# Sparse-attention layer of a two-layer streaming encoder: when index queries take up 1/rms, where values are projected, and which engine scales late softmaxes

## The chip, the cores and the metric

The kernel runs on one core of a Trainium2 chip. Its time is device microseconds of one execution, measured over several executions. A profile records one execution, and every row of a view comes from that one.

The engines have names of their own in the views: PE is TensorE (matmuls), PEld its weight loads, DVE is VectorE, ACT is ScalarE, POOL is GpSimd, SP is SyncE, which issues most transfers here. A q behind a name is the engine's queue of DMA issues.

## The reference, cut to what matters

One inference step over 512 prompt frames and 64 sample frames goes through two layers: a pooling mixer with an MLP, then sparse attention with an MLP. The change lies in the attention. Each query ranks the keys with a small indexer (8 heads of 64), keeps the best 256 at most, and attends to these with 16 heads in 4 groups.

```python
p = rmsnorm(x, g) @ w_in            # q 1024, k 256, v 256, qi 512, ki 64, wi 8
q, k, qi, ki = rope(q), rope(k), rope(qi), rope(ki)
wi = p[..., -8:] * 8 ** -0.5
logits = einsum('bthd,bsd->bths', qi, ki) * 64 ** -0.5
score = einsum('bths,bth->bts', relu(logits), wi)
_, idx = top_k(where(adm, score, NEG), n_sel)
s = einsum('btgrd,btkgd->btgrk', qg, k[idx]) * 64 ** -0.5
p = softmax(where(valid, s, NEG))
o = einsum('btgrk,btkgd->btgrd', p, v[idx])
return o @ w_o
```

The projections are linear, so the factor 1/rms of each frame can be left out of x and multiplied in later. relu is also linear in a positive factor: relu(r * y) is r * relu(y).

## The kernel before, in words

Activations lie transposed, 128 features by 576 frames (512 prompt, then 64 sample). To keep precision every matmul operand is split in a high and a low part (`wh`/`wl` for weights, two halves of `xs` for activations), and each product is three matmuls. A matmul over 576 frames runs as two of 288. Weights come in blocks as `raw` tiles; the high part is a cast on ACT (L190), the low part a subtraction (L191) on DVE, or on POOL where `next_block(sub=pool)` or the kind of block says so. A scheduler places all instructions when the kernel is built: each engine gets one fixed order, and runs it in order, each instruction waiting for its inputs and buffers.

The attention layer is `attention` (L1099 on). In order of the code:

- Four blocks give the index queries (`pj` in PSUM). Blocks 0 and 1 are copied to SBUF by ACT (`copies`); statistics of the norm are started, and during the last block `spread()` (L1204) broadcasts 1/rms to `rb` and multiplies it into the rotation tables `cs` (POOL, L1211) and `sn` (DVE, L1212). `rope` (L1141) rotates a pair of blocks: four multiplies and two sums. `rope_qi(0, copies=...)` rotates the first four heads from the copies, `rope_qi(1, started=...)` the last four from PSUM (L1156). Each splits the result in two parts and sends it through DRAM to `qi` by SP (L1180 and L1185).
- Between the two stands the projection of index keys and weights (`pki`). `turnable` holds the weights times 1/rms (L1230); it is transposed by PE (L1247) to `wi`. The key gets the scaled tables.
- Then K and the four groups of q are projected and rotated, most of it on POOL (L1161 to L1170). Between their matmuls `pace()` lets in index scores from step `PACE_FROM` on (L1273, relu on ACT at L1274, weighted sum on DVE from L1277).
- `top_k` finds, for four blocks of queries of 192, 320, 448 and 576 keys, the mask: rounds of MAX8 (L1291) and MATCH_REPLACE8 (L1292), then a threshold (L1293) and two transfers that lay the mask out by 128 rows (L1295, L1296).
- Values are projected (L1527): five tiles `v` of 24 matmuls, each evicted by ACT with the factor `r` (L1530).
- `steps()` runs 40 units (query block i of 5, key group g of 4, pair of heads s of 2). i from 0 to 3 are prompt blocks of 128 queries with (i+1)*128 keys; i = 4 is the sample with 576 keys. `scores` of a unit runs three units (`AHEAD`) before its `transpose`. `softmax` is one DVE pass with the mask (L1311) and an exponential on ACT (L1312) that also sums the row. From i = 2 on `over` scales p by 1/sum: POOL raises the sum to -1 (L1318) and multiplies (L1320). For i below 2 the scaling comes after the values, on DVE. PE transposes p (L1367, L1372), ACT copies it to `pT`, and PE multiplies it with V (L1399, L1405).
- From unit 18 on, every other step runs one block of the output projection for the first 256 frames (`wa`, in `ahead_out`), with its lower splits on POOL.
- At the end POOL adds these to x, reloaded from DRAM (L1545), and the output projection of the other 320 frames (`wo`) follows.

Of the kernel before, what the change touches and what calls it, by code (L numbers as in the profile page):

```python
# [16 lines left out]
P = 128  # L17
D = 1024
KT = D // P
TP = 512  # L20
# [18 lines left out]
PACE_FROM = 12  # L39
# [18 lines left out]
def pool_dsa_kernel(ctx: ExitStack, tc: tile.TileContext, a, o):  # L58
# [1040 lines left out]
    def attention(parts):  # L1099
# [42 lines left out]
        def rope(fast, started=(), cast=act.copy, copies=()):  # L1142

            pts = list(started)
            while len(pts) < 2 and not copies:
                pt = psum("pj")
                project(pt, next_block(), xs, between)
                pts.append(bank_halves(pt))
            a2, b2 = (tmp("rp", "rp", 4) for _ in range(2))
            a1, b1 = copies or (tmp("rp", "rp", 4) for _ in range(2))  # L1150
            eng = dve if fast else pool
            if fast and not copies:
                pa, pb = pts
                for out, pt, by in ((a1, pa, cs), (a2, pa, sn), (b2, pb, sn), (b1, pb, cs)):
                    for t, half in pt:
                        dve.tensor_tensor(halves(out)[:, half], t, halves(by)[:, half], ALU.mult)  # L1156
            else:
                for out, pt in zip((a1, b1), pts):
                    for t, half in pt:
                        turned[:] = [act.copy(halves(out)[:, half], t).ins]  # L1160
                eng.tensor_tensor(a2, a1, sn, ALU.mult)  # L1161
                eng.tensor_tensor(a1, a1, cs, ALU.mult)
                eng.tensor_tensor(b2, b1, sn, ALU.mult)
                eng.tensor_tensor(b1, b1, cs, ALU.mult)
            eng.tensor_tensor(a1, a1, b2, ALU.subtract)
            eng.tensor_tensor(b1, b1, a2, ALU.add)
            st = [pair_slot("b", "st") for _ in range(2)]
            for j, t in enumerate((a1, b1)):
                cast(st[j][:, 0], t)
                low = pool.tensor_tensor(st[j][:, 1], t, f32(st[j][:, 0]), ALU.subtract)  # L1170
            turned.append(low.ins)
            return (a1, b1), st

        def rope_qi(g, **ready):

            _, st = rope(True, **ready)
# [20 lines left out]
        copies = []  # L1197
        for i in range(2):
            pt = psum("pj")
            project(pt, next_block(), xs)  # L1200
            copies.append(tmp("rp", "rp", 4))
            act.copy(halves(copies[i]), pt[:, :, :HT])
            if i == 0:
                norm.stats()  # L1204

        def spread():

            for k in range(KT):
                if k == SPREAD_AT:
# [5 lines left out]
        started = []  # L1215
        for i in range(2):
            pt = psum("pj")
            project(pt, next_block(), xs, spread() if i else iter(()))
            started.append(bank_halves(pt))
        r = norm.r  # L1220
        between = iter(())
        qi = const([P, NIDX, TP], "qi", F32R, phase["queries"])
        pool.memset(f32(qi[:, :, TP - P:TP - TS]), 0.0)
        rope_qi(0, copies=copies)
        pki = psum1("ki"), psum1("ki")
        project(pki, next_block(), xs)
        rope_qi(1, started=started)
        turnable = tmp("wi")
        for h, pk in enumerate(pki):
            dve.scalar_tensor_tensor(halves(turnable[0:32])[:, h], pk[64:96, :HT], NIDX ** -0.5, halves(norm.rb[0:32])[:, h], ALU.mult, ALU.mult)  # L1230
        t1, t2, ki = tmp("t1"), tmp("t2"), tmp("ki")
# [82 lines left out]
        def over(sums, *heads):  # L1314
# [3 lines left out]
            pool.tensor_tensor(rs, sums, inverse[:, :n], ALU.pow)  # L1318
            for h, p in enumerate(heads):
                pool.tensor_scalar(p, p, rs[:, h:h + 1], 1.0, ALU.mult, ALU.mult)  # L1320

        class Unit:
# [5 lines left out]
            def scores(self):  # L1328
# [6 lines left out]
                if i < 4:  # L1335
# [8 lines left out]
                    if i >= TURNED:  # L1344
                        over(self.group.sums[:, 2 * s:2 * s + 2], self.pr[:, 0], self.pr[:, 1])
                else:
# [6 lines left out]
                    over(self.group.sums[:, s:s + 1], self.pr)  # L1353
# [95 lines left out]
        def ahead_out():  # L1449

            for m in range(KT):
# [3 lines left out]
                with behind(turned):  # L1455
                    w = next_block(sub=pool)
# [11 lines left out]
        def steps():  # L1468
# [3 lines left out]
            for u in range(-AHEAD - 2, total + 2):  # L1472
# [5 lines left out]
                if 0 <= u + AHEAD < total:  # L1478
# [3 lines left out]
                    v.scores()  # L1482
                if 0 <= u - 1 < total:
# [5 lines left out]
                yield  # L1489

# [12 lines left out]
        act.activation(small(8, "e1", 1), wi[:, 1], AF.Exp)  # L1503
# [15 lines left out]
        wv = [next_block(), next_block()]  # L1519
        for i in range(5):  # L1520
            n = P if i < 4 else TS
            pt = psum1("v")
            for k in range(KT):
                wh, wl = wv[k // 4][k % 4 // 2]
                sl = slice((k % 2) * 256, (k % 2 + 1) * 256)
                for j, (part, wt) in enumerate(((0, wh), (1, wh), (0, wl))):
                    pe.matmul(pt[:n, :256], xs[k][:, part, i * P:i * P + n], wt[:, sl],  # L1527
                              start=(k == 0 and j == 0), stop=(k == KT - 1 and j == 2))
            vi = i if i < 4 else 8
            act.activation(V[:n, vi], pt[:n, :256], AF.Copy, scale=r[:n, i:i + 1])  # L1530
        nc.sync.dma_start(o["v_p"], V[:, 0:4])
        nc.sync.dma_start(o["v_s"], V[:TS, 8])
# [125 lines left out]
```

## Time and profile before

| | us |
|---|---|
| median of 3 runs (lowest, highest) | 1087.7 (1087.55, 1088.82) |
| the profiled execution's own time | 1087.32 |
| span of its profile | 1085.1 |
| PE busy in the span | 1053.3 (97%) |
| DVE busy | 893.0 (82%) |
| ACT busy | 631.3 (58%) |
| POOL busy | 258.2 (24%) |

The span leaves out 2.2 us that lie around it. The attention layer runs from about 409 to 696 us of the span, between the two MLPs. A busy time is the time in which an engine executed something; a wait shows in brackets behind the instruction that ended it, with what released it. PE's instructions are pipelined, so a busy PE may still run at a lower clock, and each window gives the clock that was granted.

### The profile page before, as it was taken

Reading aid. Unit: us, or ns where it says so; the run is one execution under the profiler, and the core shown is the slowest. Engines: PE = TensorE matmul, PEld = TensorE weight load, DVE = VectorE, ACT = ScalarE, POOL = GpSimd, SP = SyncE. Lnnn points to the kernel's source line nnn. Section 1 sums busy time; section 2 is a strip of 40 time slices with the busy share of each in tenths; the row PEclk is TensorE's granted clock in tenths of the full one; section 3 lists DMA queues with packets and bytes.
Section 4 is the critical chain, followed back from the end, with each engine's and each line's share of the span. In section 5 each row is a group of like instructions: output and inputs, shape, how many; then the busy total and the mean of one; then the engine's idle time right before and its main releaser. Section 6 shows DMA issues by size and latency. Waiting matters only on the chain.

```text
span 1085.1 us, 21735 instructions
## 1 busy us (share of the span) xinstructions
PE 1053.3 (97%) x7978; PEld 1028.0 (95%) x7978; DVE 893.0 (82%) x1822; ACT 631.3 (58%) x1262; POOL 258.2 (24%) x285
## 2 busy tenths in 40 slices
PE   8999999999999999989989999999999999999996
PEld 8999999999999999989988787999999999999995
DVE  7889889879979996859999433779989879978984
ACT  8556457447547764434378765646556547647741
POOL 3200111111111101576516784000111111111101
PEclk9999999999999999999989999999999999999999
DMA  8333666676676655675352443533666676576522
GB/s 250 91 103 89 170 166 151 175 167 164 147 184 165 158 169 173 183 194 162 104 172 79 141 138 109 159 98 90 161 164 163 160 174 168 146 182 162 127 60 88
DMA packets 98427, 160.17 MB, mean 148 GB/s; under 512 B 15777, under 2 KB 29584, under 8 KB 98320
## 3 DMA queue, kind: packets, MB, share of 16 engines
q1 hardware_dynamic: 71120, 112.30, 33.1%
q0 software_dynamic: 15840, 28.84, 16.8%
q10 hardware_dynamic: 11360, 17.63, 5.1%
q8 instruction: 63, 1.03, 0.4%
q14 instruction: 44, 0.36, 0.1%
HBM read 142.99 MB, written 12.72 MB: 143 GB/s over the span
## 4 chain that ended last, share of the span: by engine, by line
PE 85%; issue 4%; DVE 4%; POOL 2%; ACT 2%; DMA 2%; SPq 0%; DVEq 0%; ACTq 0%; POOLq 0%
PE b L522 32%; PE c L522 16%; PE up L320 9%; PE a L522 8%; PE pj L320 7%; PE wo L320 3%; PE wa L320 2%; PE pb L1066 1%; PE o L1399 1%; PE dn L320 1%; PE pt L1367 1%; PE ix L1269 1%; PE sc L1341 1%; PE ix L1273 1%; POOL p L1320 1%
## 5 line engine op out<-in xcount | busy, mean ns | idle before, releaser
L190 ACT CAST wh<-raw 128x512 fp32r<-128x512 f32 x316 | 194.6, 619 | 222.5 <-PE b L522 62.9
L191 DVE TENSOR_TENSOR wl<-raw,wh 128x512 fp32r<-128x512 f32 x284 | 199.1, 703 | 40.6 <-ACT wh L190 36.7
L522 PE MATMUL b<-u,wh 128*128 128x288 f32 x992 | 203.3, 296 | 2.3 <-ACT a L559 1.9
L522 PEld LDWEIGHTS b<-u,wh 128*128 128x128 f32 x992 | 159.6, 188 | 4.3 <-ACT a L559 3.1
L190 ACT CAST wh<-sum 128x512 fp32r<-128x512 f32 x165 | 102.3, 620 | 95.8 <-PE b L522 41.9
L522 PE MATMUL b<-u,wl 128*128 128x288 f32 x496 | 145.8, 295 | 0.4 <-DVE wl L191 0.4
L191 DVE TENSOR_TENSOR wl<-sum,wh 128x512 fp32r<-128x512 f32 x165 | 112.1, 685 | 22.4 <-ACT wh L190 20.8
L253 POOL DMA_DIRECT2D sum<-in_w_down x31 | 27.1, 893 | 331.0 <-DMA sum<-in_w_down 105.6
L522 PE MATMUL c<-u,wh 128*128 128x288 f32 x496 | 102.7, 296 | 0.0
L522 PEld LDWEIGHTS b<-u,wl 128*128 128x128 f32 x496 | 93.5, 189 | 0.6 <-DVE wl L191 0.6
L320 PE MATMUL up<-xs,wh 128*128 128x288 f32 x512 | 89.4, 296 | 0.2
L488 DVE TENSOR_TENSOR u<-v,u 128x576 fp32r<-128x576 f32 (+3 forms) x106 | 83.0, 785 | 2.1 <-ACT u L485 1.6
L522 PEld LDWEIGHTS c<-u,wh 128*128 128x128 f32 x496 | 79.7, 188 | 1.4 <-ACT wh L190 1.1
L522 PE MATMUL b<-xt,wh 128*128 128x288 f32 x384 | 77.7, 296 | 0.0
L522 PE MATMUL b<-xs,wh 128*128 128x288 f32 x384 | 77.2, 295 | 0.0
L485 ACT CAST u<-v 128x576 fp32r<-128x576 f32 (+3 forms) x106 | 73.7, 699 | 3.2 <-DVE v L509 2.2
L320 PEld LDWEIGHTS up<-xs,wh 128*128 128x128 f32 x512 | 74.7, 188 | 1.0 <-DVE v L474 0.6
L522 PE MATMUL c<-u,wl 128*128 128x288 f32 x248 | 73.1, 295 | 0.0
L253 POOL DMA_DIRECT2D sum<-in_w_up x24 | 20.7, 863 | 203.3 <-DVE wl L191 68.5
L320 PE MATMUL pj<-xs,wh 128*128 128x288 f32 x352 | 62.2, 295 | 0.0
L1311 DVE CUSTOM_DVE_ANT_0 p<-sc,mask 128x128 f32<-128x128 f32 (+4 forms) x72 | 34.5, 513 | 33.6 <-POOL p L1320 11.6
L522 PEld LDWEIGHTS b<-xt,wh 128*128 128x128 f32 x384 | 61.6, 188 | 0.0
(298 smaller groups left out, 2759.9 us busy)
## 6 DMA issues: line engine op xcount, KB each, us to landing
raw<-in_w_up SPq DMA_DIRECT2D x128, 256.0 KB, 3.0
raw<-in_w_down SPq DMA_DIRECT2D x128, 256.0 KB, 2.8
raw<-in_w_o ACTq DMA_DIRECT2D x32, 256.0 KB, 3.0
sum<-in_w_down SPq DMA_DIRECT2D x31, 256.0 KB, 2.9
sum<-in_w_down POOLq DMA_DIRECT2D x31, 256.0 KB, 4.4
raw<-in_w_down POOLq DMA_DIRECT2D x31, 256.0 KB, 5.0
raw<-in_w_in ACTq DMA_DIRECT2D x30, 256.0 KB, 2.8
sum<-in_w_up SPq DMA_DIRECT2D x24, 256.0 KB, 3.1
```

The source lines that it names most:

```text
L190: act.copy(h, src)
L191: (sub or how["sub"]).tensor_tensor(l, src, f32(h), ALU.subtract)
L253: pool.dma_start(s1, odd[:, 512:], accum_op=ALU.add)
L320: pe.matmul(pt[h][:, :m] if isinstance(pt, tuple) else pt[:, h, :m], wt, xs[k][:, part, c:c + m], start=(k == 0 and i == 0), stop=(k == n ...
L485: return act.copy(u[:, f, 0], v[:, f])
L488: return dve.tensor_tensor(u[:, f, 1], v[:, f], f32(u[:, f, 0]), ALU.subtract)
L522: ins = pe.matmul(bank[:, :HT], wt, ut, start=first and j == 0 and i == 0, stop=j == 3 and i == 2, skip_group_check=True)
L1066: pe.matmul(pt[:, c0:c0 + rhs.shape[1]], lhs, rhs, start=n == 0, stop=n == len(steps) - 1)
L1269: pe.matmul(pf[:, :m], qi[:, h, t0:t0 + P], keys[:, part, at:at + m], start=part == 0 and keys is kis, stop=part == 1 and keys is cki)
L1273: pe.matmul(pf[:rows, :m], q[:, h], kis[:, part, :m], start=part == 0, stop=part == 1)
L1311: dve.tensor_tensor_reduce(dst, src, mask, -0.125, 3e38, ALU.add, ALU.min, nm)
L1320: pool.tensor_scalar(p, p, rs[:, h:h + 1], 1.0, ALU.mult, ALU.mult)
```

## The change

1. Index queries. All four blocks are rotated directly from PSUM with the plain tables, each pair right behind its own two projections; `copies` goes. 1/rms is spread at the first step of the index-key projection. Since the queries now lack their 1/rms, the index weights get the factor a second time, by a new POOL multiply of 32x576. The load of the exponential's table moves there too.
2. `PACE_FROM` goes from 12 to 10.
3. Values are projected inside `steps()` at unit 0, behind the scores of the first units. Their PSUM tiles come from the stage of the units.
4. `over` with i above 2: reciprocal and multiply on DVE instead of power and multiply on POOL. i = 2 stays on POOL.
5. The lower splits of the last four blocks of `wa` go from POOL to DVE.

```diff
-PACE_FROM = 12
+PACE_FROM = 10
...
-        def rope(fast, started=(), cast=act.copy, copies=()):
+        def rope(fast, started=(), cast=act.copy):
...
-            if fast and not copies:
+            if fast:
...
-        copies = []
+        between = iter(())
+        qi = const([P, NIDX, TP], "qi", F32R, phase["queries"])
+        pool.memset(f32(qi[:, :, TP - P:TP - TS]), 0.0)
+        started = []
         for i in range(2):
             pt = psum("pj")
             project(pt, next_block(), xs)
-            copies.append(tmp("rp", "rp", 4))
-            act.copy(halves(copies[i]), pt[:, :, :HT])
+            started.append(bank_halves(pt))
+        rope_qi(0, started)
+        started = []
+        for i in range(2):
+            pt = psum("pj")
+            project(pt, next_block(), xs)
+            started.append(bank_halves(pt))
             if i == 0:
                 norm.stats()
+        rope_qi(1, started)
...
-                if k == SPREAD_AT:
+                if k == 0:
                     rb = norm.spread()
...
-            project(pt, next_block(), xs, spread() if i else iter(()))
...
-        rope_qi(0, copies=copies)
-        pki = psum1("ki"), psum1("ki")
-        project(pki, next_block(), xs)
-        rope_qi(1, started=started)
+        pki = psum1("ki"), psum1("ki")
+        project(pki, next_block(), xs, spread())
...
+        act.activation(small(8, "e1", 1), norm.rb[:, :8], AF.Exp)
         turnable = tmp("wi")
         for h, pk in enumerate(pki):
             dve.scalar_tensor_tensor(halves(turnable[0:32])[:, h], pk[64:96, :HT], NIDX ** -0.5, halves(norm.rb[0:32])[:, h], ALU.mult, ALU.mult)
+        pool.tensor_tensor(turnable[0:32], turnable[0:32], norm.rb[0:32], ALU.mult)
...
-        def over(sums, *heads):
+        def over(late, sums, *heads):
...
-            pool.tensor_tensor(rs, sums, inverse[:, :n], ALU.pow)
+            if late:
+                dve.reciprocal(rs, sums)
+            else:
+                pool.tensor_tensor(rs, sums, inverse[:, :n], ALU.pow)
             for h, p in enumerate(heads):
-                pool.tensor_scalar(p, p, rs[:, h:h + 1], 1.0, ALU.mult, ALU.mult)
+                (dve if late else pool).tensor_scalar(p, p, rs[:, h:h + 1], 1.0, ALU.mult, ALU.mult)
...
-                        over(self.group.sums[:, 2 * s:2 * s + 2], self.pr[:, 0], self.pr[:, 1])
+                        over(i > 2, self.group.sums[:, 2 * s:2 * s + 2], self.pr[:, 0], self.pr[:, 1])
...
-                    w = next_block(sub=pool)
+                    w = next_block(sub=pool if m < KT // 2 else dve)
...
+                if u == 0:
+                    project_values()
...
-        act.activation(small(8, "e1", 1), wi[:, 1], AF.Exp)
```

`project_values` is the loop of before, from `wv = [next_block(), next_block()]` to the two stores of V, word for word.

Three places of the order change with it. The first is DVE at the rotation of index queries. `pj` are projected queries in PSUM, `rp` the rotated ones, `sn` and `cs` the tables, `rba` 1/rms. Before, after the statistics:

```order
L1212 TENSOR_TENSOR sn<-sn,rba_5701 128x576
L1161 TENSOR_TENSOR rp_5730<-rp_5508,sn 128x576
L1163 TENSOR_TENSOR rp_5731<-rp_5593,sn 128x576
L1162 TENSOR_TENSOR rp_5508<-rp_5508,cs 128x576
L1164 TENSOR_TENSOR rp_5593<-rp_5593,cs 128x576
L191 TENSOR_TENSOR w_6165<-raw_6078,w_6165 128x512
L1165 TENSOR_TENSOR rp_5508<-rp_5508,rp_5731 128x576
L1166 TENSOR_TENSOR rp_5593<-rp_5593,rp_5730 128x576
L1156 TENSOR_TENSOR rp_5820<-pj_5595,cs 128x576
L1156 TENSOR_TENSOR rp_5818<-pj_5595,sn 128x576
```

Now, ahead of the statistics (L392 and L394 belong to them):

```order
L1155 TENSOR_TENSOR rp_5573<-pj_5453,cs 128x576
L1155 TENSOR_TENSOR rp_5576<-pj_5453,sn 128x576
L191 TENSOR_TENSOR wl_5604<-raw_5515,wh_5603 128x512
L1155 TENSOR_TENSOR rp_5574<-pj_5510,sn 128x576
L1155 TENSOR_TENSOR rp_5575<-pj_5510,cs 128x576
L191 TENSOR_TENSOR wl_5610<-raw_5522,wh_5609 128x512
L1164 TENSOR_TENSOR rp_5573<-rp_5573,rp_5574 128x576
L392 TENSOR_SCALAR ms_912_5669<-st_5663 128x4
L392 TENSOR_SCALAR ms_912_5669<-st_5663 64x1
L394 RECIPROCAL r_915_5672<-rt_913_5670 128x5
L1165 TENSOR_TENSOR rp_5575<-rp_5575,rp_5576 128x576
```

The first rotation stood behind the scaled table `sn`; now it stands ahead of the statistics from which the table's factor is made.

The second is PE where values meet the first units. `v` are value tiles, `sc` scores, `pt` transposed softmaxes. Before:

```order
L1527 MATMUL v_7009<-wh_6800,xs_5428 64x256 x2
L1527 MATMUL v_7009<-wl_6801,xs_5428 64x256
L1341 MATMUL sc_7052<-k_6048,q_7046 128x256 x4
L1341 MATMUL sc_7064<-k_6048,q_7046 128x256 x4
L1341 MATMUL sc_7155<-k_6048,q_7049 128x256 x4
L1367 MATMUL pt_7166<-ident,p_7051 128x128 x2
```

Now (`v_7050` is the first value tile, `v_7076` the second):

```order
L1506 MATMUL v_7050<-wl_6800,xs_5428 128x256
L1506 MATMUL v_7076<-wh_6717,xs_5397 128x256 x2
L1506 MATMUL v_7076<-wl_6718,xs_5397 128x256
L1506 MATMUL v_7076<-wh_6717,xs_5397 128x256 x2
L1344 MATMUL sc_6895<-k_6057,q_6889 128x256 x4
L1344 MATMUL sc_6907<-k_6057,q_6889 128x256 x4
L1344 MATMUL sc_6998<-k_6057,q_6892 128x256 x4
L1506 MATMUL v_7076<-wl_6718,xs_5397 128x256
```

The first scores stood behind all 120 value matmuls, and stand behind 29 of them now.

The third is the scaling of units with i = 3. `sums` are the row sums, `over` their inverses. Before, on POOL:

```order
L1318 TENSOR_TENSOR over_1398_7990<-sums_1348_7803,inverse 128x2
L1320 TENSOR_SCALAR p_7978<-p_7978,over_1398_7990 128x512 x2
L191 TENSOR_TENSOR wl_8259<-raw_8147,wh_8258 128x512
L1318 TENSOR_TENSOR over_1406_8024<-sums_1348_7803,inverse 128x2
L191 TENSOR_TENSOR wl_8265<-raw_8153,wh_8264 128x512
L1320 TENSOR_SCALAR p_8012<-p_8012,over_1406_8024 128x512 x2
```

Now, on DVE, between its softmaxes (L1311, whose second row reads out the maximum):

```order
L1319 RECIPROCAL over_1398_7989<-sums_1348_7802 128x2
L1323 TENSOR_SCALAR p_7977<-p_7977,over_1398_7989 128x512 x2
L191 TENSOR_TENSOR wl_8258<-raw_8146,wh_8257 128x512
L1311 ISA p_8083,nm_8089<-sc_8084,mask_5878 128x512
L1311 ISA nm_8089 128x1
L1311 ISA p_8083,nm_8092<-sc_8084,mask_5878 128x512
L1311 ISA nm_8092 128x1
L1319 RECIPROCAL over_1406_8023<-sums_1348_7802 128x2
L191 TENSOR_TENSOR wl_8264<-raw_8152,wh_8263 128x512
L1323 TENSOR_SCALAR p_8011<-p_8011,over_1406_8023 128x512 x2
```

The scalings and the splits `wl` left POOL's queue and stand in DVE's, among the softmaxes of later units.

## What was predicted before the run

> **What bounds the kernel now.** I read the windows of the attention layer first. In each row stand start and end, the length, then the busy time of PE, of weight loading, VectorE (DVE), ScalarE (ACT) and GpSimd (POOL), the granted clock of PE, the DMA share and GB/s.
>
> ```profile
> span 1085.1 us, 21735 instructions
> ...
> 446.50:473.60 27.10, 23.71 (x179) 23.11 (x180) 16.36 (x30) 11.40 (x24) 18.56 (x14) 1.00 0.74 214
> 473.60:530.00 56.40, 56.40 (x418) 56.13 (x417) 54.08 (x136) 25.65 (x53) 33.32 (x24) 1.00 0.61 163
> 530.00:548.80 18.80, 15.85 (x134) 15.65 (x133) 18.18 (x40) 5.92 (x11) 14.03 (x11) 0.97 0.41 128
> 548.80:601.30 52.50, 51.02 (x414) 46.52 (x414) 49.99 (x180) 42.36 (x135) 19.70 (x28) 0.95 0.37 105
> 601.30:606.80 5.50, 5.50 (x58) 4.99 (x56) 0.42 (x1) 2.69 (x5) 1.76 (x2) 1.00 0.80 248
> 606.80:648.20 41.40, 39.48 (x363) 34.45 (x361) 16.60 (x46) 30.48 (x67) 36.33 (x45) 1.00 0.38 118
> 648.20:665.80 17.60, 13.57 (x113) 10.35 (x112) 5.53 (x13) 12.01 (x30) 12.23 (x17) 0.90 0.39 136
> ```
>
> Three different limits stand here. From 446.5 to 473.6 PE lacks 3.4 us and VectorE is half idle. From 473.6 to 601.3 VectorE is busy 54.08 + 18.18 + 49.99 = 122.3 of 127.7 us: the top-k searches and, from 548.8, the softmaxes. From 606.8 POOL is the busiest after PE, 36.33 + 12.23 = 48.6 of 59.0 us.
>
> The timeline shows the places (start, length, engine, line, operation, tiles, idle before and its releaser).
>
> ```profile
> 446.50 3.30 PE L320 MATMUL pj<-xs,w 128*128 128x288 f32 x23 [1.25 <-DVE rp L1156]
> 457.22 0.25 PE L1273 MATMUL ix<-kis,qi 128*64 128x192 f32 x1
> ...
> 459.97 0.35 PE L1273 MATMUL ix<-kis,qi 128*64 128x192 f32 x2
> ...
> 463.79 2.91 SPq L1185 DMA_DIRECT2D qi<-qi  x6
> 470.88 0.90 PE L1273 MATMUL ix<-kis,qi 128*64 128x192 f32 x8 [3.38 <-DMA out_k<-rp]
> 473.59 0.35 DVE L1291 MAX8 m<-mask 64x8 f32<-64x192 f32 x1
> 530.16 0.39 PE L1527 MATMUL v<-wh,xs 128*128 128x256 f32 x2
> 539.30 0.63 DVE L1291 MAX8 m<-mask 128x8 f32<-128x448 f32 x1
> 543.76 0.62 PE L1341 MATMUL sc<-k,q 128*128 128x256 f32 x4
> 547.33 1.94 PE L1341 MATMUL sc<-k,q 128*128 128x256 f32 x8 [2.95 <-ACT V L1530]
> 548.79 0.27 DVE L1311 CUSTOM_DVE_ANT_0 p<-sc,mask 128x128 f32<-128x128 f32 x1
> 600.81 0.46 DVE L1293 TENSOR_SCALAR mask<-mask 128x576 f32<-128x576 f32 x1
> 606.80 0.69 DVE L1311 CUSTOM_DVE_ANT_0 p<-sc,mask 128x512 f32<-128x512 f32 x1 [3.94 <-DMA mask<-mask]
> ```
>
> PE stands still 1.25 us until VectorE has rotated index queries 2 and 3, and 3.38 us before index scores of heads 4 to 7. The trace names out_k there; those matmuls read kis and qi, and the last qi writes are issued on SP until 466.7, so I read it as qi landing. The first top-k operation follows at 473.59. Values run from 530.16 to 543.76, and the first softmax only comes at 548.79.
>
> **Part 1: index queries and weights.** Both PE stalls have their cause removed: queries 0 to 3 are rotated straight from PSUM, behind their own projections, and their stores leave earlier. Taken away are 1.25 + 3.38 = 4.6 us, so values would start at 525.5. Of the top-k I expect more. The scores of heads 0 to 3 were done at 459.97 + 0.35 = 460.3 and then waited for the other four, whose eight matmuls led to the top-k in 473.59 - 470.88 = 2.7 us. With those following at once the top-k begins at 463.0, or 461.8 with the 1.25 us of PE: 11.8 us earlier at best. The number I use is below; 11.8 only caps it.
>
> The change adds one POOL multiply of 32x576, bounded by the nearest POOL multiply of 128x576:
>
> ```profile
> 437.04 1.53 POOL L1211 TENSOR_TENSOR cs<-cs,rba 128x576 f32<-128x576 f32 x1 [0.31 <-ACT rba L351]
> 437.20 1.98 DVE L1212 TENSOR_TENSOR sn<-sn,rba 128x576 f32<-128x576 f32 x1
> 439.22 0.76 DVE L1161 TENSOR_TENSOR rp<-rp,sn 128x576 f32<-128x576 f32 x1
> ```
>
> I take nothing for it, since PE has projection matmuls to run before the weights are transposed; if that cover fails it is up to 1.5 us of the 4.6. The rotation's multiplies are four on VectorE before and after (PSUM instead of an ACT copy), the copies leave ScalarE, and the earlier 1/rms moves to a stretch where PE has the ki projection: nothing. PACE_FROM 12 to 10 only lets index scores in earlier; nothing by itself.
>
> **Part 2: values amid the first units.** The 120 value matmuls (13.6 us from 530.16 to 543.76, 0.113 each) are not removed. In the new PE order 29 of them precede the first eight score matmuls, so the first softmax's scores are there at 525.5 + 29 x 0.113 + 0.6 = 529.4. On VectorE the first softmax stands behind the 10th of the 16 rounds of the third top-k; before it stood behind the 15th. The 10th round of before ended at 539.3 (the MAX8 row above begins the 11th). So if VectorE arrives there when the scores do, its order is 539.3 - 529.4 = 9.9 us ahead, under the cap of 11.8. Both ends: 4.6, when VectorE gains only what PE gains, and PE's own ceiling. PE's lack between 446.5 and 601.3 is 3.39 + 2.95 + 1.48 = 7.8, with the 1.25 before that 9.1; by the clock column (0.97 of 18.8, 0.95 of 52.5) another 0.6 + 2.6 = 3.2 went to a lower clock, in all 12.3:
>
> ```profile
> 548.00:555.00 7.00, 6.62 (x32) 5.93 (x32) 7.00 (x33) 4.98 (x19) 0.26 (x1) 0.55 0.81 237
> ```
>
> That row shows where: right after the 2.95 us wait PE ran at about half clock, so value matmuls placed there also cover the clock. 9.9 would leave PE only 2.4 us of slack while VectorE too is near full. Two nearly full engines wait for each other now and then, so I take **9.0**. It reaches the end of the mask (600.81) and, the mask's DMA trip of 6.0 us unchanged, the softmax at 606.80. PE has look-ahead output projection for that trip, as it had (5.50 of 5.50 busy).
>
> **Part 3: late scalings.** These groups of 606.8 to 665.8 (busy us, mean ns, then idle before) carry it.
>
> ```profile
> L191 POOL TENSOR_TENSOR wl<-raw,wh 128x512 fp32r<-128x512 f32 x9 | 11.7, 1295 | 0.0
> L1320 POOL TENSOR_SCALAR p<-p,over 128x512 f32<-128x512 f32 x16 | 11.0, 710 | 0.1
> L1320 POOL TENSOR_SCALAR p<-p,over 128x576 f32<-128x576 f32 x8 | 6.3, 790 | 0.7
> L1545 POOL TENSOR_TENSOR x<-x,wo 128x256 f32<-128x256 f32 x8 | 5.8, 737 | 6.0 <-DMA x<-xd 6.0
> L1318 POOL TENSOR_TENSOR over<-sums,inverse 128x2 f32<-128x2 f32 x8 | 5.7, 714 | 0.2
> L307 POOL TENSOR_TENSOR ck<-raw,ck 128x512 fp32r<-128x512 f32 x4 | 5.2, 1304 | 0.1
> L1318 POOL TENSOR_TENSOR over<-sums,inverse 128x1 f32<-128x1 f32 x8 | 4.9, 610 | 4.2 <-ACT p L1312 4.2
> ...
> L1424 DVE RECIPROCAL rs<-sums 128x4 f32<-128x4 f32 x8 | 1.3, 167 | 0.0
> ...
> L1312 ACT ACTIVATE p<-p,nm 128x512 f32<-128x512 f32 x16 | 11.5, 720 | 2.7 <-DVE nm L1311 2.7
> L1312 ACT ACTIVATION_READ_ACCUMULATOR p<-p,nm 128x1 f32 x24 | 4.5, 189 | 0.0
> ...
> DVE p L1311 <- POOL p L1320: 11.6, 3, 4.4
> DVE p L1311 <- PE sc L1341: 4.5, 3, 2.8
> DVE p L1311 <- PE sc L1351: 2.7, 2, 1.8
> ...
> L191 DVE TENSOR_TENSOR wl<-raw,wh 128x512 fp32r<-128x512 f32 x284 | 199.1, 703 | 40.6 <-ACT wh L190 36.7
> ```
>
> From POOL go 11.0 + 6.3 + 5.7 + 4.9 = 27.9 us of scaling and 8 lower splits x 1.295 = 10.4: 48.6 falls to 10.3, and its 6.0 us wait for x<-xd no longer holds scalings queued behind it. VectorE had 16.60 + 5.53 = 22.1. It gets 24 scalings at 0.46 us at most (the 128x576 TENSOR_SCALAR at 600.81) = 11.0, 16 reciprocals x 0.167 = 2.7 and 8 splits x 0.70 = 5.6: 41.4. Its 11.6 us of waiting for p on POOL end. What is late next? VectorE runs in order, and in the new order a scaling often stands directly behind its own unit's softmax, so it waits for the exponential, 0.72 + 0.19 = 0.91 us, with the next softmax queued behind it. If all 16 units did so, VectorE would need 41.4 + 16 x 0.91 = 56.0. PE had 39.48 + 13.57 = 53.1 busy, of which 0.10 x 13.57 = 1.4 went to the lower clock, so PE's floor is 51.7. The stretch lies between 51.7 and 59.0 if nothing else joins. I take 54.5, nearer VectorE's upper end than PE's floor: a gain of **4.5**, ends 0 and 7.3.
>
> A rule speaks against this part. In the rows of part 1 a VectorE multiply of two SBUF operands took 1.98 us beside a POOL multiply and a like one 0.76 alone. The Trainium skill, page "SBUF — State Buffer", section "Who interferes with whom", says that VectorE and GpSimd share one port pair that is locked exclusively: a VectorE tensor_scalar in a 2-port mode, or an operation with two SBUF inputs, and a GpSimd operation shut each other out entirely. The trace agrees in size (1.98 against 0.76). By that rule the late scalings would pay for whatever POOL still does, and the sum would come out at the 1086.7 of the third rival below, against the 1074.2 that I reach.
>
> **Sum.** 1087.3 of the profiled execution (2.2 around its span) - 9.0 - 4.5 = 1073.8. The median of the runs is 0.4 higher: **1074.2**.
>
> **Rivals.**
> *Late scalings gain nothing (1078.7).* VectorE's waits for exponentials and the port take what POOL gave: 1087.3 - 9.0 + 0.4. For it: 56.0 is near 59.0. Against: POOL's 11.6 us of holding VectorE really go.
> *Only the stalls are saved (1078.6).* VectorE does not get its top-k started earlier than PE's 4.6 allow, or the value evictions, queued on ScalarE behind exponentials of the first units, hold the values: -4.6 - 4.5 + 0.4. For it: VectorE is 97% busy from 473.6 on, so only an earlier start helps. Against: it was busy 16.36 of 27.10 us before that.
> *VectorE and POOL shut each other out in the late stretch (1086.7, no change).* POOL's remaining 5.8 of x and 5.2 of ck are two-operand work like the multiply that stretched VectorE's from 0.76 to 1.98 us. Added to VectorE's 56.0 they make the stretch 67.0, 8.0 longer: 1087.3 - 9.0 + 8.0 + 0.4. The page named above would have it so. Against it: it needs all 11.0 us to fall on VectorE's work, which fills two thirds of the stretch.
> *The late stretch becomes serial on VectorE (1093.9, slower).* Each scaling waits its exponential (56.0), POOL blocks it for 11.0 as above, and the waits for scores (4.5 + 2.7 = 7.2) stay, as later scalings hold the PSUM release: 74.2 us, 15.2 more than now, less the 9.0: 1087.3 + 6.2 + 0.4. It decides against the change from 59.0 + 9.0 + 2.2 = 70.2 on. Against it: the orders put some scalings one unit later, and the exponential of a first head runs beside the second softmax.
> That the order does not change as described is no rival here: the rows of it show it.
>
> **Chances.** Forecast 0.56, nothing from the late scalings 0.20, only the stalls 0.14, shut out 0.04, serial 0.04, elsewhere faster 0.02. A measurement can tell about 0.2% (2.2 us) from no change. Faster 0.56 + 0.20 + 0.14 + 0.02 = 0.92, same 0.04, slower 0.04. The ends: PE's ceilings, 12.3 + 7.3 = 19.6, give 1068.1, less 1 for the spread of the runs (1087.55 to 1088.82): **1067**. Upward both middle rivals are held, and part of their meeting (both: 1087.3 - 4.6 + 0.4 = 1083.1): **1082**.
>
> **What would show it.** Right: no wait of PE over 1 us before index scores of heads 4 to 7; first top-k by about 465; first softmax near 530 to 532, with value matmuls between; the 128x576 mask finished near 592; the stretch from the first 128x512 softmax to the first wo matmul near 54.5, with no wait of VectorE for POOL. Wrong: a first softmax later than 535, a long PE wait for a value tile's eviction, wl or p releases by VectorE that PE waits for in the late stretch, or VectorE scalings far over 0.46 us beside POOL.

## The result, and the profile after

The changed kernel takes 1072.5 us (median of four runs, 1071.3 to 1073.9) against 1087.6 for the kernel before in the same measurement: a ratio of 0.9863, interval 0.9844 to 0.9882. The forecast was 1074.2, range 1067 to 1082. Its profiled execution has a span of 1071.1 us, 14.0 less. The windows that answer to those of before, with edges at the start of the top-k, the start and end of the values, the last threshold, the first 128x512 softmax behind it, and the first `wo` matmul at 650.7:

```profile
span 1071.1 us, 21712 instructions
...
446.50:463.06 16.56, 15.53 (x122) 15.03 (x121) 13.14 (x26) 6.85 (x16) 10.42 (x8) 1.00 0.66 178
463.06:526.00 62.94, 62.94 (x467) 62.67 (x466) 57.83 (x149) 27.87 (x57) 41.84 (x29) 1.00 0.62 168
526.00:542.00 16.00, 16.00 (x141) 16.00 (x140) 15.12 (x48) 8.92 (x26) 11.02 (x9) 1.00 0.27 87
542.00:591.45 49.45, 48.11 (x416) 44.07 (x415) 47.38 (x159) 39.45 (x122) 23.12 (x30) 1.00 0.45 127
591.45:596.84 5.39, 5.39 (x52) 5.05 (x52) 0.45 (x3) 2.31 (x4) 1.81 (x2) 1.00 0.77 236
596.84:638.00 41.16, 39.42 (x348) 33.60 (x347) 30.24 (x86) 32.75 (x72) 10.06 (x11) 0.96 0.42 123
638.00:650.70 12.70, 12.03 (x121) 9.81 (x121) 7.96 (x22) 10.26 (x27) 1.56 (x3) 1.00 0.51 171
```

PE no longer stands still from 463.06 to 542, the half clock behind the values is gone (1.00 in both rows), and POOL has 10.06 + 1.56 = 11.6 us in the late stretch where it had 48.6. The timeline gives the events:

```profile
452.06 0.40 PE L1247 MATMUL wi<-ident,wi 32*64 32x32 f32 x4 [0.63 <-POOL wi L1230]
...
463.06 0.35 DVE L1291 MAX8 m<-mask 64x8 f32<-64x192 f32 x1
...
526.00 0.39 PE L1506 MATMUL v<-wh,xs 128*128 128x256 f32 x2
...
529.29 1.52 PE L1344 MATMUL sc<-k,q 128*128 128x256 f32 x12
...
529.94 0.29 DVE L1311 CUSTOM_DVE_ANT_0 p<-sc,mask 128x128 f32<-128x128 f32 x1
...
591.45 0.45 DVE L1293 TENSOR_SCALAR mask<-mask 128x576 f32<-128x576 f32 x1
596.84 0.69 DVE L1311 CUSTOM_DVE_ANT_0 p<-sc,mask 128x512 f32<-128x512 f32 x1 [4.94 <-issue]
...
603.31 1.38 PE L1370 MATMUL pt<-ident,p 128*128 128x128 f32 x8 [1.25 <-DVE p L1323]
```

The top-k begins 10.5 us earlier, values 4.2, the first softmax 18.9, the last mask's threshold 9.4, and the first softmax behind it 10.0. The last row is the longest wait of PE that is left: it ends with a late scaling on VectorE, which stands behind a split and the two softmaxes of a later unit.

### The profile page after: what moved, and what is told of

The parts are those of the page before. It is cut to its first block, busy times and chain, and to the rows that moved or that the text cites. A ratio compares the mean times of both kernels' runs of the same rounds, so it can differ in the third digit from the quotient of the medians.

```text
span 1071.1 us, 21712 instructions
## 1 busy us (share of the span) xinstructions
PE 1048.7 (98%) x7978; PEld 1024.5 (96%) x7978; DVE 908.5 (85%) x1870; ACT 630.9 (59%) x1260; POOL 226.1 (21%) x238
## 4 chain that ended last, share of the span: by engine, by line
PE 91%; DVE 3%; DMA 2%; ACT 2%; issue 1%; POOL 0%; SPq 0%; DVEq 0%; ACTq 0%; POOLq 0%
PE b L522 33%; PE c L522 16%; PE up L320 9%; PE a L522 8%; PE pj L320 7%; PE wo L320 2%; PE wa L320 2%; PE sc L1344 2%; PE o L1402 1%; PE pt L1370 1%; PE pb L1066 1%; DMA raw<-in_w_in 1%; PE dn L320 1%; PE v L1506 1%; PE ix L1269 1%
## 5 line engine op out<-in xcount | busy, mean ns | idle before, releaser
L191 DVE TENSOR_TENSOR wl<-raw,wh 128x512 fp32r<-128x512 f32 x292 | 203.3, 698 | 33.6 <-ACT wh L190 26.8
L522 PEld LDWEIGHTS b<-xs,wh 128*128 128x128 f32 x384 | 61.2, 188 | 0.0
```

The source lines that it names most:

```text
L191: (sub or how["sub"]).tensor_tensor(l, src, f32(h), ALU.subtract)
L522: ins = pe.matmul(bank[:, :HT], wt, ut, start=first and j == 0 and i == 0, stop=j == 3 and i == 2, skip_group_check=True)
```

## The experiments

Beside each time I keep a book of what PE lost in the attention layer, from the first matmul of its projections to the first of the second MLP: in seven windows, length less busy time, plus length times what the clock column lacks to 1.00. For the kernel before these are the four windows that carry nearly all of it: up to the values, the 28 us behind their start (the ramp in what follows), and the late stretch in two pieces:

```profile
409.44:530.20 120.76, 116.13 (x865) 114.62 (x864) 94.73 (x205) 53.19 (x105) 61.19 (x44) 1.00 0.60 172
530.20:558.20 28.00, 24.15 (x181) 23.15 (x181) 26.06 (x77) 13.21 (x39) 14.03 (x11) 0.88 0.52 157
...
606.80:655.62 48.82, 43.93 (x394) 37.91 (x393) 19.42 (x51) 35.58 (x80) 43.55 (x54) 0.98 0.46 146
655.62:665.42 9.80, 8.74 (x77) 6.51 (x77) 2.71 (x8) 6.52 (x17) 5.01 (x8) 0.94 0.05 16
```

They read 4.6 up to the values, 3.85 + 3.36 = 7.2 in the ramp, and 4.89 + 0.98 + 1.06 + 0.59 = 7.5 in the late stretch; with 0.6 elsewhere 19.9 us. In the table all kernels are read the same way. The layer's length less PE's losses is 263.4 to 266.2 us in each of them: to within 2.8 us, what a kernel gains is what PE no longer loses.

| kernel | ratio to before, interval | layer | lost in all | up to values | ramp | late |
|---|---|---|---|---|---|---|
| before | 1 | 286.2 | 19.9 | 4.6 | 7.2 | 7.5 |
| changed | 0.9863 (0.9844 to 0.9882) | 272.1 | 7.3 | 1.0 | 0.8 | 4.2 |
| values only | 0.9958 (0.9943 to 0.9973) | 282.4 | 16.8 | 6.0 | 6.0 | 4.2 |
| queries only | 0.9912 (0.9895 to 0.9929) | 275.4 | 9.3 | 0.4 | 4.5 | 2.5 |
| late only | 0.9965 (0.9950 to 0.9980) | 280.9 | 15.7 | 5.9 | 6.8 | 2.4 |
| late undone | 0.9874 (0.9859 to 0.9889) | 272.1 | 7.4 | 0.3 | 0.7 | 5.1 |
| x added last | 0.9968 (0.9950 to 0.9987) | 283.0 | 17.7 | 5.1 | 7.4 | 3.8 |
| POOL kept busy | 0.9900 (0.9868 to 0.9932) | 276.1 | 11.4 | 2.0 | 0.9 | 7.2 |
| values undone | 0.9907 (0.9871 to 0.9943) | 274.0 | 8.9 | 0.9 | 5.9 | 1.0 |
| paced from 12 | 0.9870 (0.9838 to 0.9902) | 271.6 | 8.1 | 0.1 | 1.3 | 6.0 |
| changed, again | 0.9861 (0.9842 to 0.9881) | 269.2 | 4.1 | 0.1 | 0.5 | 2.3 |
| late undone, again | 0.9878 (0.9859 to 0.9896) | 272.3 | 7.5 | 1.3 | 0.5 | 4.4 |
| two small edits | 0.9862 (0.9843 to 0.9882) | 270.9 | 5.3 | 1.0 | 0.7 | 2.3 |

Between two executions of one program the part up to the values moves by about 1 us (1.0 and 0.1 of the changed kernel); the clock column has two digits, which alone leaves 0.6 us either way in a window of 120 us. The late part moves more: over the five profiles whose late code is the changed one (changed, changed again, late only, values undone, paced from 12) it runs from 1.0 to 6.0. So a single late entry does not carry an argument by itself; below it stands beside times, or beside waits that the traces name.

My theory after the result was the forecast's: the first half gains by VectorE's earlier start, the late stretch by POOL's relief. The rivals were that PE's own waits carry the gain, and that the late scalings bring nothing.

**Values only.** The block that projects values moves into `steps()`; all else as before.

```diff
+                if u == 0:
+                    project_values()
```

> The kernel before with values projected amid the first units and nothing else changed. Theory (the gain of the attention's first half is VectorE's earlier start on the top-k): VectorE is as full as before and starts its top-k no earlier, so the first softmax comes near 539, where its new place in VectorE's order is reached, the same work follows, and the end of the last mask moves by the 2 to 3 us that VectorE lost around 530 to 555: about 1085. Rival (the gain is PE's ramp: its 2.95 us wait for a value eviction and its 3.2 us at a lower clock): about 1081.5.

1082.4 against 1087.0. The first softmax came where the theory had it, but the mask's end went the other way:

```profile
477.48 0.55 DVE L1277 TENSOR_SCALAR mask<-ix,wi 128x320 f32<-128x320 f32 x1 [2.07 <-ACT ix L1274]
...
538.51 0.27 DVE L1311 CUSTOM_DVE_ANT_0 p<-sc,mask 128x128 f32<-128x128 f32 x1
...
603.32 0.45 DVE L1293 TENSOR_SCALAR mask<-mask 128x576 f32<-128x576 f32 x1
...
609.30:651.25 41.95, 38.53 (x360) 33.67 (x358) 16.34 (x45) 33.16 (x74) 39.39 (x49) 1.00 0.45 135
```

The threshold is 2.5 us later than before and the ramp still loses 6.0; in the book the gain stands in the late stretch, 7.5 to 4.2. Both views failed: with VectorE late, moving values does not fill the ramp, and the mask does not come earlier. Of the 2.5 us, 1.3 are older than the move: VectorE waited 2.07 us at 477.48 for an index score from ScalarE where it had waited 0.54 before, and was 1.3 us late (529.50 for 528.17) in the top-k round ahead of the moved matmuls. Whether the early softmaxes push the top-k by the other 1.2 is not shown.

**Queries only.** Rotation with plain tables, 1/rms in the weights, pacing from 10; values and late scalings as before.

```diff
-        rope_qi(0, copies=copies)
+        rope_qi(0, started)
...
+        pool.tensor_tensor(turnable[0:32], turnable[0:32], norm.rb[0:32], ALU.mult)
```

> The kernel before with the index queries rotated with plain tables, 1/rms in the weights and index scores paced from 10; values and late scalings as before. Theory (VectorE's earlier start): the top-k begins near 463, PE reaches values near 525.5 and the first scores near 539.7, so the first softmax comes near 540.5 instead of 548.8 and the mask's end moves by about 8: 1079.5. Rival (only PE's two stalls are saved, and without the moved values VectorE's lead is lost in waiting for the first scores): 1083.

1077.0 against 1087.0, 10.0 less, more than either. Top-k at 462.4, values at 525.3, first softmax at 540.8 and threshold at 591.7 are as the theory had them (8 to 9 us). PE's stalls lose 4.2 less and the ramp 2.7 less; the late stretch gives 5.0, though POOL still does all its work there:

```profile
525.30:553.30 28.00, 25.14 (x197) 23.76 (x196) 25.02 (x80) 14.93 (x47) 14.06 (x11) 0.94 0.53 151
...
597.70:644.71 47.01, 45.42 (x425) 39.75 (x424) 17.93 (x48) 37.01 (x84) 43.99 (x53) 1.00 0.53 161
644.71:654.51 9.80, 8.92 (x85) 6.79 (x85) 2.81 (x9) 7.71 (x22) 5.98 (x10) 1.00 0.21 73
```

POOL is busy 43.99 + 5.98 us of 56.8, as before, and PE loses 1.59 + 0.88. So POOL's sum of work was not what held the stretch. (From the first 128x512 softmax to the first `wo` matmul it is still 57.6 us, with more of PE's work in it: 425 + 85 matmuls in the two windows, 394 + 77 before.)

**Late only.** `over` on VectorE for i above 2 and four blocks' lower splits on VectorE, in the kernel before.

```diff
-                        over(self.group.sums[:, 2 * s:2 * s + 2], self.pr[:, 0], self.pr[:, 1])
+                        over(i > 2, self.group.sums[:, 2 * s:2 * s + 2], self.pr[:, 0], self.pr[:, 1])
...
-                    w = next_block(sub=pool)
+                    w = next_block(sub=pool if m < KT // 2 else dve)
```

> The kernel before with the scalings of units with i above 2 and the last four blocks' lower splits on VectorE, nothing else changed. Theory (POOL's queue bounds the stretch after the last mask): 4 us less, 1083.6, all of it after the last mask. Rival (the stretch is shorter in the changed kernel for another reason, such as the weights being there earlier): no change, 1087.6.

1083.1 against 1087.0: the 4 us of the theory, and in the book they stand in the late stretch (7.5 to 2.4).

**Late undone.** The same edit reversed, in the changed kernel.

```diff
-                        over(i > 2, self.group.sums[:, 2 * s:2 * s + 2], self.pr[:, 0], self.pr[:, 1])
+                        over(self.group.sums[:, 2 * s:2 * s + 2], self.pr[:, 0], self.pr[:, 1])
```

> The changed kernel with its late scalings and the lower splits back on POOL. Theory: the first half keeps its 10 us, the stretch after the last mask takes 58 to 59 us again: 1076.5. Rival (the moved scalings bring nothing by themselves): 1072.5.

1073.0, where the theory wanted 1076.5: the rival's number. From the first 128x512 softmax (596.11) to the first `wo` matmul (650.30) it is 54.2 us, where the theory wanted 58 to 59, though POOL is busy 47.8 us in its two windows. Alone the edit brings 4 us; on top of the rest it brings hardly any. What PE still waits for on POOL stands at the start of the stretch:

```profile
601.11 0.33 PE L1367 MATMUL pt<-ident,p 128*128 128x128 f32 x1 [2.51 <-POOL p L1320]
604.36 0.33 PE L1367 MATMUL pt<-ident,p 128*128 128x128 f32 x1 [1.23 <-POOL p L1320]
```

With the scalings on VectorE that place had the wait of 1.25 us shown above, and 3.67 us in "paced from 12". Beside each other in one later measurement, changed and undone:

> The changed kernel once more, on the chip of the next two, so that they can be set beside it: 1072.5, ratio to the kernel before 0.986.

> The changed kernel with late scalings and lower splits on POOL, once more beside the changed kernel. Theory (with the first half moved, POOL no longer waits long for the reload of x, and the late scalings are worth only the difference of PE's lost time): within 1.5 us of the changed kernel. Rival (they are worth the 4 us that they bring by themselves, and the first run hid it): 1076, 3.5 us above the changed kernel of this job.

1071.0 and 1072.6. The two pairs give 0.5 and 1.7 us, the second just over the 1.5 of the theory. In it the slowest of four executions of the changed kernel (1071.9) is still below the fastest of the other (1072.2), so a difference is there, some 1 to 2 us; the 3.5 us of the rival would need the extremes of both.

**x added last.** What stood in POOL's queue before? At 641.5 the next in POOL's order was an addition of x, whose reload had been issued on SP at 639.84:

```profile
639.84 0.33 SPq L1543 DMA_DIRECT2D x<-xd  x1
...
640.92 0.57 POOL L1318 TENSOR_TENSOR over<-sums,inverse 128x1 f32<-128x1 f32 x1
646.01 1.42 POOL L1545 TENSOR_TENSOR x<-x,wo 128x256 f32<-128x256 f32 x2 [4.52 <-DMA x<-xd]
647.38 1.29 POOL L191 TENSOR_TENSOR wl<-raw,wh 128x512 fp32r<-128x512 f32 x1
648.65 0.75 POOL L1320 TENSOR_SCALAR p<-p,over 128x576 f32<-128x576 f32 x1
...
649.45 0.77 PE L1372 MATMUL pt<-ident,p 128*128 128x128 f32 x5 [1.10 <-POOL p L1320]
653.39 1.97 PE L1405 MATMUL o<-pT,V 128*64 128x128 f32 x16 [1.48 <-ACT pT L1378]
```

A split and the scalings of the last units stood behind it. PE then waited 1.10 us for the first of these scalings, 0.39 for the next, and 1.48 for the copies behind them, 3.0 in all. The experiment orders the additions behind the last scaling, in the kernel before.

```diff
-        for m in range(KT):
-            pool.tensor_tensor(x[m][:, :2 * P], x[m][:, :2 * P], ahead[m], ALU.add)
+        with behind(scaled):
+            for m in range(KT):
+                pool.tensor_tensor(x[m][:, :2 * P], x[m][:, :2 * P], ahead[m], ALU.add)
```

> The kernel before, with the eight POOL additions of the early output projection to x placed behind the last unit's scaling in POOL's order; the scalings stay on POOL and nothing is left out. Theory (what PE lost at the end of the late stretch came from one addition that stood in POOL's queue and waited 4.5 us for the reload of x, with splits and scalings behind it): that loss goes, some 4 us, 1083. Rival (it came from the sum of POOL's work in the stretch, 48.6 us, of which 5.8 move): at most 1.5 us, 1085.5.

1084.4 against 1087.1, 2.7 less (by the interval 1.4 to 5.4): between the two numbers, 1083 and 1085.5. The trace is clearer: those three waits are gone, and the only one that PE shows from 617 to its first `wo` matmul is of 0.67 us. In the book the late stretch loses 3.8 instead of 7.5; what is left of it are waits of 1.79 and 1.23 us for scalings at its start, as in "late undone". In "late undone" POOL waited 1.8 us in all for the reload:

```profile
POOL x L1549 <- DMA x<-xd: 1.8, 2, 1.4
```

Before it was 6.0, 4.5 of them at once. The other two kernels with their scalings on POOL agree: the longest such wait of the late stretch is 1.1 us in "queries only", and 1.5 in "values only", where the reload is issued at 640.04, as before, but POOL comes to the addition at 643.8 instead of 641.5. So the late scalings, the earlier first half and the later addition each take away the loss behind that one wait, which can be taken once. Only the addition's edit names the cause by itself; why a shift of the first half makes POOL come to the addition late enough was read from the traces, not tried.

**POOL kept busy.** The changed kernel with 48 idle multiplications on POOL beside the late scalings, into the dead table `cs`; the outputs' computation is whole.

```diff
+                if late:
+                    for _ in range(2):
+                        pool.tensor_scalar(cs[:, :p.shape[-1]], cs[:, :p.shape[-1]], rs[:, h:h + 1], 1.0, ALU.mult, ALU.mult)
```

> The changed kernel, with two extra POOL multiplications for every late scaling, into a table that nobody reads any more, so that POOL works some 34 us more in the late stretch, beside VectorE's scalings, and nobody waits for the results. Theory (only waiting for POOL costs, not its running): no change, within 1 us of 1072.5. Rival (VectorE and POOL shut each other out at their shared port): VectorE's scalings and splits grow by up to half of POOL's added time, and the stretch by 5 us or more: 1077 or above.

1076.4, some 4 us more than the changed kernel: the rival's side, though the intervals of the two ratios overlap. The forms of VectorE in the late stretch, first of the changed kernel, then of this one:

```profile
L1311 DVE CUSTOM_DVE_ANT_0 p<-sc,mask 128x512 f32<-128x512 f32 x16 | 10.3, 687 | 6.9 <-issue 4.9 <-PE sc L1344 2.0
L191 DVE TENSOR_TENSOR wl<-raw,wh 128x512 fp32r<-128x512 f32 x11 | 7.6, 687 | 3.0 <-ACT wh L190 3.0
L1323 DVE TENSOR_SCALAR p<-p,over 128x512 f32<-128x512 f32 x16 | 7.5, 511 | 0.2
...
L1323 DVE TENSOR_SCALAR p<-p,over 128x576 f32<-128x576 f32 x8 | 4.2, 519 | 0.2
```

```profile
L1323 DVE TENSOR_SCALAR p<-p,over 128x512 f32<-128x512 f32 x16 | 12.6, 829 | 0.2
L1311 DVE CUSTOM_DVE_ANT_0 p<-sc,mask 128x512 f32<-128x512 f32 x16 | 10.2, 679 | 4.8 <-issue 4.8
L191 DVE TENSOR_TENSOR wl<-raw,wh 128x512 fp32r<-128x512 f32 x11 | 8.4, 767 | 2.8 <-ACT wh L190 2.7
...
L1323 DVE TENSOR_SCALAR p<-p,over 128x576 f32<-128x576 f32 x8 | 5.5, 692 | 0.2
...
L1326 POOL TENSOR_SCALAR cs<-cs,over 128x512 f32<-128x512 f32 x32 | 26.6, 831 | 2.9 <-DVE over L1319 0.4
```

Scalings grow from 511 to 829 ns and from 519 to 692, splits from 687 to 767; 7.2 us of VectorE time for 41 us of POOL's (26.6 and 14.8). Softmaxes, whose scores come from PSUM, do not grow (687 and 679). The Trainium skill, page "SBUF — State Buffer", section "Who interferes with whom", states that a VectorE tensor_scalar in a 2-port mode and a VectorE operation with two SBUF inputs contend with GpSimd, and that one with at most one SBUF input outside these modes does not. The trace agrees in kind: the scalings (tensor_scalar) and the splits (two SBUF inputs) grow, the softmax pass, with its mask as the one SBUF input, does not. Whether the scalings ran in a 2-port mode no run here shows. Nor is it shown that this growth is all of the 4 us: the fuller queue of POOL also held others up, ScalarE 1.9 and VectorE 1.4 us behind a POOL split of `ck` by the profile, waits that the changed kernel does not have.

**Values undone.** The changed kernel with values ahead of all units.

```diff
-                if u == 0:
-                    project_values()
```

> The changed kernel with values projected ahead of all units again, as before; index queries and late scalings as changed. Theory (PE's lost time is what counts; with the queries alone PE still lost 4.5 us in the ramp after the values, and 2.5 in the late stretch): values in the units are worth the ramp, 3 to 4 us, so 1076. Rival (VectorE's early start already gives all of it): 1072.5.

1077.0 against 1072.5, close to the theory's 1076; the intervals of the ratios just overlap. The ramp tells them apart, 5.9 against 0.8:

```profile
525.60:553.60 28.00, 25.46 (x191) 24.02 (x189) 24.25 (x75) 14.43 (x45) 14.06 (x11) 0.88 0.51 149
```

```profile
526.00:554.00 28.00, 27.23 (x236) 26.55 (x235) 26.72 (x94) 19.37 (x63) 14.36 (x11) 1.00 0.52 158
```

45 more matmuls fit in the same 28 us. This kernel also shows what a wait for the reload costs when no scaling stands behind it:

```profile
610.35 1.82 POOL L1547 TENSOR_TENSOR x<-x,wo 128x256 f32<-128x256 f32 x2 [4.74 <-DMA x<-xd]
```

PE is busy all of the 14 us around it (602 to 616) and loses 1.0 us in the whole late stretch.

**Paced from 12.**

```diff
-PACE_FROM = 10
+PACE_FROM = 12
```

> The changed kernel with index scores paced from step 12 again instead of 10. Theory (the start of the top-k is set by the queries' landing and by the transposed weights, not by the pacing): the first top-k begins at most 1.5 us later and the time stays within 1 us of 1072.5. Rival (the pacing gives the top-k its start): the first softmax comes 2 us later or more, and the time is 1074.5 or above.

1073.4, with the first top-k at 463.5: no difference that can be told, as the theory had it, though the first softmax came at 531.4, 1.5 us later.

**Two small edits.** The weights' second factor on VectorE, the last splits back on POOL.

```diff
-        pool.tensor_tensor(turnable[0:32], turnable[0:32], norm.rb[0:32], ALU.mult)
+        dve.tensor_tensor(turnable[0:32], turnable[0:32], norm.rb[0:32], ALU.mult)
...
-                    w = next_block(sub=pool if m < KT // 2 else dve)
+                    w = next_block(sub=pool)
```

> The changed kernel with two small edits: the second factor of the index weights on VectorE instead of POOL, and the lower splits of the last four blocks back on POOL, while the late scalings stay on VectorE. Theory (PE's remaining waits are 0.6 us for the weights and 1.4 us for late scalings that stand behind other VectorE work): 1 to 1.5 us less than the changed kernel, near the limit of what can be told. Rival (VectorE has room in both places, and POOL's two-operand splits stretch its scalings): no change, or 1 us more.

1071.2 beside 1071.0: no change, the rival's side. VectorE was spared eight splits, some 5.5 us, and paid 2.6 of them back: with splits on POOL its 128x512 scalings took 675 ns instead of 511. None of the kernels tried is shown to beat the changed one.

## Why the prediction was right, point by point

The time was right by parts that were not. "Late undone" has the first half's edits alone and is 13.7 to 14.0 us faster than the kernel before, where the forecast gave the first half 9.0; the late scalings add 0.5 to 1.7, where it gave them 4.5. That the two errors cancel in the sum is luck.

**Part 1.** Values were to start at 525.5 and started at 526.0; the top-k's cap of 11.8 us earlier was nearly used, 10.5. The POOL multiply taken at nothing, with up to 1.5 if its cover failed, took 1.41 us and let PE wait 0.63: the cover failed by a half. Pacing at nothing held within what the runs can tell.

**Part 2.** The scores were to be there at 529.4; their matmuls began at 529.29 and the softmax at 529.94. Of the 9.9 us at the softmax 9.0 were to reach the mask, and 9.4 did; the mask's transfers, taken at 6.0 us, took 5.4. The earlier mask needs the queries alone: "queries only" had its threshold at 591.7, and "values only" had it late. PE's ramp needs both edits: it lost 7.2 there before, 6.0 with the values moved alone, 4.5 with the queries alone, and 0.5 to 1.3 in every kernel with both. With the values alone PE waits behind them for softmaxes of a VectorE that is busy throughout (549 to 557 us); with the queries alone the block of values still stands ahead of the scores. The rival "only the stalls are saved" fell: top-k and mask moved by twice that. (Its "97% busy from 473.6 on" is 96% by the rows: 122.3 of 127.7 us.)

**Part 3.** The stretch from the first 128x512 softmax to the first `wo` matmul was to take 54.5 and took 650.71 - 596.84 = 53.9. The number came out and the step behind it failed. "From POOL go 27.9 us ... 48.6 falls to 10.3" is what happened, but it was not what bound the stretch: with POOL as loaded as ever, "queries only" lost 2.5 us there and "late undone" 4.4 to 5.1, against 7.5 before, and "late undone" took 54.2 us for the stretch. What the runs put in its place is the 4.5 us wait for a reload in POOL's queue with scalings behind it: 2.7 us of the time when the additions were moved. I had that wait in the sum as "its 6.0 us wait for x<-xd no longer holds scalings queued behind it", beside the work and not instead of it, and did not ask whether the first half's 9 us would shift it. The cause of the rest of what the late scalings bring by themselves stays open. So the rival "late scalings gain nothing" was wrong on the time that it gave, 1078.7, and nearly right on its subject. "VectorE and POOL shut each other out" gave POOL 11.0 us, and POOL had 11.6; what it had wrong was that all of these lengthen a VectorE that is the limit of the stretch. That VectorE's operations grow beside POOL's is shown.

VectorE came out below its sum: busy 30.24 + 7.96 = 38.2 us where I had 41.4, and 8.0 us of waits for exponentials where I allowed up to 16 x 0.91 = 14.6, so 46.2 and not 56.0. The scalings took 7.5 + 4.2 = 11.7 where I had 11.0. PE was busy 39.42 + 12.03 = 51.5 of the 53.9, so taking 54.5 for its nearness to VectorE's 56.0 was luck too. One sign of being wrong did show: PE waited for a `p` released by VectorE, the 1.25 us above. A rise that I did not foresee is the 0.75 us that PE waits for x ahead of the second MLP.

## What to carry to other kernels

Where one engine is 97% busy, book what it loses, idle time and lost clock, stretch by stretch: the rest stayed within 2.8 us from version to version, so the book shows where a gain sits. Take it from more than one execution: the late entry alone moved by 5 us here. Gains of single edits do not add, neither in the times (4.5, 10.0 and 3.9 us, and 15.1 for all) nor in the book. Before a queue's work is called the bound, look for the one instruction in it that waits with ready work behind it. Two edits that each shorten the time may remove the same wait, and two that each fill little of a stretch may fill it together.

## What the hardware showed that was not expected

The clock fell to half after waits of PE of 1.25 and 0.23 us, and did not after one of 2.51 us followed by 1.23. The first wait is in the row at 603.31 above, the second in the row that follows; those of "late undone" are at 601.11 and 604.36 above. Then come the changed kernel in 2 us windows, and "late undone":

```profile
604.92 2.00 PE L1344 MATMUL sc<-k,q 128*128 128x512 f32 x4 [0.23 <-DVE nm L1311]
```

```profile
601.00:603.00 2.00, 1.06 (x9) 0.72 (x7) 2.00 (x7) 2.00 (x7) 0.00 (x0) 1.00 0.48 95
603.00:605.00 2.00, 1.39 (x9) 0.96 (x9) 2.00 (x7) 1.60 (x4) 0.41 (x1) 1.00 0.79 191
605.00:607.00 2.00, 2.00 (x6) 1.16 (x8) 1.56 (x5) 2.00 (x5) 0.88 (x1) 0.51 0.89 338
```

```profile
599.00:601.00 2.00, 0.00 (x0) 0.00 (x0) 0.87 (x4) 2.00 (x7) 2.00 (x3) 1.00 0.44 131
601.00:603.00 2.00, 1.89 (x12) 1.57 (x12) 0.46 (x1) 1.76 (x6) 2.00 (x4) 1.00 0.40 131
603.00:605.00 2.00, 0.77 (x6) 0.57 (x5) 1.18 (x5) 1.99 (x3) 2.00 (x4) 1.00 0.65 112
605.00:607.00 2.00, 2.00 (x22) 1.47 (x21) 1.25 (x4) 1.47 (x5) 2.00 (x3) 1.00 0.86 307
```

In a second execution of the changed kernel the same two waits (1.26 and 0.23 us) kept the clock (1.00 in the 42.4 us around them). So a short wait may or may not cost 1.7 us of clock behind it (0.51 and 0.64 in the two windows from 605 to 609); what decides it stays open here.

The POOL multiply of 32x576 took 1.41 us, as long as POOL's multiplies of 128x576 in the same profile take on three of their lines: here fewer partitions saved nothing.

```profile
L1161 POOL TENSOR_TENSOR rp<-rp,cs 128x576 f32<-128x576 f32 x4 | 5.7, 1432 | 0.0
...
L1230 POOL TENSOR_TENSOR wi<-wi,rba 32x576 f32<-32x576 f32 x1 | 1.4, 1407 | 0.0
```
